# Attention scores of a decoder layer as pairs of 64-row products instead of stacked 128-row products

## The chip, the core and the metric

One core of a Trainium2 chip runs the whole program. The time is that of one execution on the device, in microseconds (us); the figure for a kernel is the median of its runs. TensorE is the matrix engine, VectorE and ScalarE work on tiles of 128 partitions, GpSimd does lighter vector work, and SP and ScalarE issue most of the transfers (DMA). In the profile they are PE (products), PEld (loads of the stationary operand into PE), DVE, ACT, POOL and SP.

## The reference

One layer of a hybrid decoder for a prompt of 512 tokens and 8 single new tokens, width 1024, 16 heads of 64, all in 32-bit floats. The part that matters here is the prompt's attention with a forget gate:

```
s = einsum("bqhd,bkhd->bhqk", q_i, k) * scale          # scale = 64 ** -0.5
s = s + fq_i[..., None] - Fk[:, :, None, :]            # sums of log forget gates
s = where(kpos <= qpos, s, -inf)                       # causal
p = softmax(s, axis=-1)
o = einsum("bhqk,bkhd->bqhd", p, v)
```

q, k and v are products of the normed input h with columns of w_in. Around this stand a recurrent branch A with its projection w_proj_a, attention of the new tokens over a paged cache, a merge, and a gated feed-forward part.

## The kernel before

Everything lies transposed: features on partitions, tokens (512 of the prompt and 8 new ones, NP and NT = 520) along the free axis. A 32-bit product is made of three cheaper ones: each operand x is split into a rounded part hi and a rest lo = x - hi, and w·a is taken as whi·ahi + wlo·ahi + whi·alo (part_product, line 305). The tokens are cut in two halves of 260 columns (HALVES). A projection (product, line 326) makes 8 x 3 products of 260 columns for each half and gives the half to a function that empties the PSUM bank. TensorE has 8 such banks; scores, transposes and projections all draw from them. Tiles in SBUF mostly come from one heap of 60 slots.

Attention goes through 8 head pairs i. The heads of a pair lie one above the other in one 128-partition tile: head a has the 64 partitions HEADS[a] of q and k.

- k_product(i) (line 1265) projects k. For head a it makes a tile ks[a] of 128 partitions: the rounded part of k on the head's own 64 partitions (line 1273, two casts per half), the rest k - hi on the other 64 (line 1277, two subtractions per half). Line 1274 copies k out for storing.
- q_load(i) (line 1285) fetches q from a scratch area in device memory: for each head its 64 rows go to both halves of a tile, four transfers of 64 partitions, on SP's queue.
- q_split(i) (line 1291) makes from each head's doubled tile a rounded part qq[a] and a rest ql[a], scaled by -1/8: two ScalarE and two VectorE instructions of 128 x 512.
- scores(i, blocks) (line 1349) makes, for a query block b of 128 tokens and each head, one score tile of 128 x (128 b + 128) in a bank of its own. Since qq[a] holds the rounded q twice and ks[a] holds k's rounded part and rest, the product of 128 rows qq·ks (line 1362) is qhi·khi + qhi·klo; the second, ql·ks (line 1363), adds qlo·khi + qlo·klo. VectorE then adds the decay rows and takes the minimum (line 1369), ScalarE the exponential (line 1370), VectorE the reciprocal of the sums (line 1372), and ScalarE or GpSimd scales (line 1376).
- turn(i, a) (line 1378) transposes the probabilities (line 1385) and splits them (lines 1389, 1390); values(i) (line 1409) multiplies with v (line 1419).

The order is written out by hand. In the loop of line 1503, step i does the k product of pair i + 1 with the turns of v's tokens between its halves, the first turn of pair i, then the v product of i + 1, with turn(i, 1) and scores(i + 1, (0, 1)) between its halves, then values(i) and scores(i + 1, (2, 3)). Between these, `at` (line 1499) issues work for the new tokens: reads of cache pages, products of their probabilities with cached values (line 946, four tiles of 32 columns of the array side by side), and small steps of their softmax. Scores of pair 0 stand inside and behind branch A's last projection (lines 1489, 1493); k_product(0) and q_load(0) stand before branch A's projections (lines 1480, 1481), and q_split(0) inside them. Weights are split a given time ahead of their use (split_upto, line 226): a cast on ScalarE (line 250) and a subtraction on VectorE (line 252). Pages of cached keys are multiplied and summed on VectorE (lines 857, 858).

Two other forms of product matter. lru_gates of the recurrent branch (line 1121) already uses row tiles: each of two heads' 64 rows has an array tile of its own, named by tile_position (line 1130). And the products of line 946 use column tiles.

Of the kernel before, what the change touches and what calls it, by code (L numbers as in the profile page):

```python
# [8 lines left out]
F32 = mybir.dt.float32  # L9
F32R = mybir.dt.float32r  # L10
I32 = mybir.dt.int32
AF = mybir.ActivationFunctionType
ALU = mybir.AluOpType
# [5 lines left out]
NP = 512  # L19
# [3 lines left out]
DH = 64  # L23
# [44 lines left out]
def kernel(ctx, tc, xT, par1, par, gates, b_f, cst, cse, own, cache_k, cache_v, cache_lf, pt,  # L68
# [3 lines left out]
    pe, act, dve, pool, sp = nc.tensor, nc.scalar, nc.vector, nc.gpsimd, nc.sync  # L72
# [9 lines left out]
    def slot(name, cols=NT, dt=F32, parts=128):  # L82
        return heap.tile([parts, cols], dt, name=name, tag="slot")

    def bank(name, parts=128, cols=512):
        return psp.tile([parts, cols], F32, name=name, tag="bank")

    def small(name, parts, cols, bufs=4):
        return sm.tile([parts, cols], F32, name=name, tag="s_" + name, bufs=bufs)
# [73 lines left out]
    for jt in range(FF // 128):  # L163
# [5 lines left out]
        for name in BLOCKS:  # L169
            units.append((c, name, 4))  # L170
            if name in JOIN[jt]:
                g, i = JOIN[jt][name]
# [12 lines left out]
    state = {"n": 0, "dma": 0, "split": 0, "load": 22, "lead": 11, "due": 0, "age": 1}  # L185
# [5 lines left out]
    def store_now(dst, src):  # L191
        act.dma_start(dst, src)
# [133 lines left out]
    def product(name, a, evac, mid=None, inside=None):  # L326
        n = begin()
        for j in range(2):
            b = bank(f"{name}_{j}")
            half_product(n, j, a, b, None if j else inside)  # L330
            evac(j, b[:, :HALF])
            if j == 0 and mid is not None:
                mid()
        run_later(n)
# [174 lines left out]
    def keep_busy(m, n, f=0):  # L509
        for _ in range(n):  # L510
            with tc.issue_after(m.ins) if m is not None else nullcontext():
                m = pe.matmul(idle[:, :HALF], lhsT=ones, rhs=x[f][:, :HALF], start=True, stop=True)
        return m
# [38 lines left out]
    def q_load(kp, raw, g3):  # L552
        sp.dma_start(raw, w_in[256 * kp:256 * kp + 256, COL_Q + 128 * g3:COL_Q + 128 * g3 + 384]
                     .rearrange("(k p) c -> p k c", p=128))

    def q_split(kp, raw, g3, behind=(), mid=None):
        hi = wp.tile([128, 2, 384], F32R, name="whi", tag="whi", bufs=3)
        lo = wp.tile([128, 2, 384], F32R, name="wlo", tag="wlo", bufs=3)
        with ExitStack() as st:
            for b in behind:  # L560
                st.enter_context(tc.issue_after(b.ins))
            for k in range(0, 2, 1 if mid else 2):
                ks = slice(k, k + 1 if mid else 2)
                state["act"] = act.copy(hi[:, ks], raw[:, ks])
                if k:
                    st.enter_context(tc.issue_after(mid()[1].ins))
                state["last"] = dve.tensor_tensor(lo[:, ks], raw[:, ks], hi[:, ks].bitcast(F32), ALU.subtract)
        for k in range(2):
            for n in range(3):
                qw[2 * kp + k, g3 + n] = hi[:, k, 128 * n:128 * n + 128], lo[:, k, 128 * n:128 * n + 128]  # L570
# [23 lines left out]
    m = None  # L594
    for f in range(KT):
        t = slot("sq1")
# [5 lines left out]
        if f > 1:  # L602
            m = keep_busy(m, 1, f)
# [43 lines left out]
    for n in range(6):  # L647
        t0, t1 = HALVES[n % 2]
# [19 lines left out]
    for n in range(6):  # L668
        t0, t1 = HALVES[n % 2]
# [176 lines left out]
    def key_sum():  # L846
        _, s, j, pg, q, half = pend.pop(0)
        r = s // 2
        c = 256 * (r % 2) + 32 * j + H * (s % 2)
        with tc.issue_after(state["last"].ins):  # L850
            if half is not None:
                b, c = 8 * (r % 2) + j, H * (s % 2) + 8 * half
                dve.tensor_tensor(pg, pg, q.unsqueeze(1).to_broadcast([128, 2, 512]), ALU.mult)
                last = dve.tensor_reduce(S[r // 2].rearrange("p (b c) -> p b c", c=32)[:, b:b + 2, c:c + 8],
                                  pg.rearrange("p j (h d) -> p j h d", d=DH), AX.X, ALU.add)
            else:
                dve.tensor_tensor(pg, pg, q, ALU.mult)  # L857
                last = dve.tensor_reduce(S[r // 2][:, c:c + H], pg.rearrange("p (h d) -> p h d", d=DH), AX.X, ALU.add)  # L858
        summed[r] += 1
        if summed[r] == 2 * NPAGE:  # L860
            chains.append([9, past_softmax(r)])
        return last
# [121 lines left out]
    qd = drp.tile([KT, 128, NT], F32, name="qd")  # L984
# [44 lines left out]
    for i in range(KT):  # L1029
        if i % 4 == 0:  # L1030
            qtp.append(bank(f"qt{i}", NS))
        if i < 6:
            t = qpart[i]
            for j, (t0, t1) in enumerate(HALVES):
                if i < 3:
                    b = qbanks[2 * i + j]
                else:
                    b = bank(f"q{i}_{j}")
# [10 lines left out]
        else:  # L1049
            t = slot("q")  # L1050
# [41 lines left out]
    HEADS = (slice(0, DH), slice(DH, 2 * DH))  # L1092
# [159 lines left out]
    sc = prm[:, :, P_SC:P_SC + 24].rearrange("p k (s n) -> p k s n", n=3)  # L1252
# [10 lines left out]
    kvs = [dict() for _ in range(KT)]  # L1263

    def k_product(i, mid=None, keys=None):
        t = slot("kt")
        ks = slot("ksA", NP, F32R), slot("ksB", NP, F32R)

        def evac(j, b):
            t0, t1 = HALVES[j]  # L1270
            n = min(t1, NP) - t0
            for a, pr in enumerate(HEADS):
                act.copy(ks[a][pr, t0:t0 + n], b[pr, :n])
            act.copy(t[:, t0:t1], b)
            for a, pr in enumerate(HEADS):
                with tc.issue_after(keys.ins) if keys else nullcontext():
                    dve.tensor_tensor(ks[a][HEADS[1 - a], t0:t0 + n], b[pr, :n], ks[a][pr, t0:t0 + n].bitcast(F32),
                                      ALU.subtract)

        product(f"k{i}", h, evac, mid)  # L1280
        kvs[i]["k"] = ks
        pool.tensor_tensor(qk8[:, NS * i:NS * i + NS], t[:, NP:], q8[:, NS * i:NS * i + NS], ALU.mult)
        store_now(kT[128 * i:128 * i + 128, :], t)

    def q_load(i):
        kvs[i]["qr"] = slot("qA", NP), slot("qB", NP)
        for a, pr in enumerate(HEADS):
            for to_ in HEADS:
                sp.dma_start(kvs[i]["qr"][a][to_], qd[i, pr, :NP])

    def q_split(i):
        qq = slot("qqA", NP, F32R), slot("qqB", NP, F32R)
        ql = slot("qlA", NP, F32R), slot("qlB", NP, F32R)
        for a in range(2):
            t = kvs[i]["qr"][a]
            act.activation(qq[a], t, AF.Copy, scale=-(DH ** -0.5))
            state["last"] = dve.scalar_tensor_tensor(ql[a], t, -(DH ** -0.5), qq[a].bitcast(F32), ALU.mult, ALU.subtract)
        del kvs[i]["qr"]
        kvs[i]["q"] = qq, ql

    def v_product(i, mid=None):
# [45 lines left out]
            fbs[hd] = f0[:, 128 * a:128 * a + 128], fmb[:, 0::3], fm[:, :384], fb  # L1347

    def scores(i, blocks):
        ks = kvs[i]["k"]  # L1350
        qq, ql = kvs[i]["q"]
        mus = small("mu", 128, 12, 4).rearrange("p (c b a) -> p c b a", c=3, b=2)
        for b in blocks:
            n = 128 * b
            for a, pr in enumerate(HEADS):
                hd = 2 * i + a
                if b == 0:
                    prob[hd] = []
                    t3 = slot("p3", 512), slot("p02", 512), slot("p1", 256)
                    pts[hd] = (t3[1][:, :128], t3[2], t3[1][:, 128:], t3[0])  # L1360
                sc = bank(f"sc{hd}_{b}")
                pe.matmul(sc[:, :n + 128], lhsT=qq[a][:, n:n + 128], rhs=ks[a][:, :n + 128], start=True, stop=False)
                pe.matmul(sc[:, :n + 128], lhsT=ql[a][:, n:n + 128], rhs=ks[a][:, :n + 128], start=False, stop=True)
                p = pts[hd][b]
                mu = mus[:, :, b - blocks[0], a]
                ins = p[:, :n + 128], sc[:, :n + 128]
                if b == 1:
                    ins = [t.rearrange("p (b c) -> p b c", b=2) for t in ins]
                dve.tensor_tensor_reduce(ins[0], fbs[hd][b], ins[1], 1.0, 3.0e38, ALU.add, ALU.min, mu[:, 0:1])  # L1369
                act.activation(p[:, :n + 128], p[:, :n + 128], AF.Exp, bias=mu[:, 0:1], scale=-1.0, accum_out=mu[:, 1:2])  # L1370
                prob[hd].append((p, mu))
        state["sums"] = dve.reciprocal(mus[:, 2], mus[:, 1])  # L1372
        for b in blocks:
            for a in range(2):
                p, mu = prob[2 * i + a][b]
                (pool.tensor_scalar(p, p, mu[:, 2:3], None, ALU.mult) if a and i + 1 < KT else act.activation(p, p, AF.Copy, scale=mu[:, 2:3]))  # L1376
# [102 lines left out]

    k_product(0)  # L1480
    q_load(0)
    decay_load(0)
    sp.dma_start(convT, conv_out)
# [19 lines left out]
    for i in range(KT):  # L1503
        last = i + 1 == KT
# [23 lines left out]
        keys = None  # L1528
        if pend:
            keys = key_sum()  # L1530
# [304 lines left out]
    for j in range(2):  # L1835
        for m in range(2 * PLAIN):
            if j == 0:
                begin(u + 3)
            b = bank(f"fi{m}_{j}")
# [90 lines left out]
```

## Time and profile before

| | |
|---|---|
| median of 3 runs | 1006.28 us (1006.1 to 1007.87) |
| the profiled execution | 1006.54 us |
| its span in the profile | 1004.9 us |
| granted TensorE clock | 0.997 |
| DMA | 206.14 MB, mean 205 GB/s |
| score products (lines 1362 and 1363) | 128, in 16 groups |

The span is the time between the first and the last instruction that the profile holds. A row of the order of time reads: start, length, engine, line, operation, output <- inputs, shape of the array that the product uses (rows * columns), shape of the moving operand, count; a bracket gives the idle time before it and what ended it. Names are the program's, with the numbers of buffers left out: sc is a score bank, ptt the transposed probabilities, pv the new tokens' value product, pa branch A's projection. Lengths of products overlap, since they are pipelined: what a product takes from TensorE's time is the step from its start to the next one's.

### The profile page before, as it was taken

To read this page: it belongs to the slowest core of one execution; us is meant where nothing else is said; L and a number is where in the kernel's file an instruction comes from. 1 tells how busy PE (TensorE), PEld (TensorE's weight loads), DVE (VectorE), ACT (ScalarE), POOL (GpSimd) and SP (SyncE) were. 2 spreads that over 40 slices of the span, in tenths; PEclk is the share of its full clock that TensorE was granted. 3 is DMA by queue.
4 is the path that set the end of the run, shared out by engine and by line. 5 is a ranking of instruction groups with operands and counts; after the bars stand their busy time and mean duration, and the time that the engine had idled before them with its cause. 6 is when DMAs were issued, how large, how long until landed. Compare 5 with 4: busy or idle time off the path is not lost.

```text
span 1004.9 us, 21556 instructions
## 1 busy us (share of the span) xinstructions
PE 985.6 (98%) x8092; PEld 915.8 (91%) x8092; DVE 791.2 (79%) x1410; ACT 564.7 (56%) x1165; POOL 339.3 (34%) x436
## 2 busy tenths in 40 slices
PE   6999999999999999999999999999999999999996
PEld 4899999999899988888888888999999999999996
DVE  5598999979999888887665444869887888888864
ACT  5434769776952587777882233544444444445453
POOL 0254121323243255654400002494343442434112
PEclk9999999999999999999999999999999999999998
DMA  9989756889879999997767994332424243233222
GB/s 315 335 271 299 235 186 184 278 261 287 277 237 378 326 311 286 303 295 231 240 223 260 333 342 139 83 106 83 117 74 126 71 120 106 64 106 106 64 64 86
DMA packets 165915, 206.14 MB, mean 205 GB/s; under 512 B 10018, under 2 KB 128434, under 8 KB 165746
## 3 DMA queue, kind: packets, MB, share of 16 engines
q1 hardware_dynamic: 149570, 153.24, 48.9%
q0 software_dynamic: 12560, 45.10, 13.4%
q10 hardware_dynamic: 3680, 6.42, 1.7%
q8 instruction: 63, 1.03, 0.4%
q14 instruction: 42, 0.34, 0.1%
HBM read 191.64 MB, written 13.09 MB: 204 GB/s over the span
## 4 chain that ended last, share of the span: by engine, by line
PE 91%; ACT 4%; DVE 2%; DMA 2%; SPq 1%; issue 1%; POOL 0%; POOLq 0%; DVEq 0%; ACTq 0%
PE fo L311 13%; PE wo L311 5%; PE gb L311 5%; PE xr L311 5%; PE pb L311 4%; PE k L311 4%; PE ga L311 4%; PE pa L311 4%; PE v L311 4%; PE gr L311 3%; PE pv L946 3%; PE po L1419 2%; PE ada L378 2%; PE ptt L1385 2%; PE fi L311 1%; PE qc L577 1%
## 5 line engine op out<-in xcount | busy, mean ns | idle before, releaser
L250 ACT CAST whi<-wraw 128x1024 fp32r<-128x1024 f32 (+1 forms) x79 | 82.0, 1040 | 96.1 <-PE pb L311 34.3
L252 DVE TENSOR_TENSOR wlo<-wraw,whi 128x1024 fp32r<-128x1024 f32 (+1 forms) x79 | 99.3, 1257 | 19.5 <-ACT whi L250 17.0
L311 PE MATMUL fo<-ach,wb 128*128 128x260 f32 x512 | 93.5, 283 | 0.0
L274 ACT CAST wb<-ws 128x512 fp32r<-128x512 f32 x72 | 44.7, 621 | 86.6 <-PE fo L311 60.2
L311 PEld LDWEIGHTS fo<-ach,wb 128*128 128x128 f32 x512 | 78.9, 188 | 0.0
L275 DVE TENSOR_TENSOR wb<-wraw,wb 128x512 fp32r<-128x512 f32 x86 | 73.8, 858 | 5.2 <-ACT wb L274 4.7
L275 DVE TENSOR_TENSOR wb<-ws,wb 128x512 fp32r<-128x512 f32 x72 | 66.2, 920 | 14.1 <-ACT wb L274 12.5
L265 POOL TENSOR_TENSOR ws<-wraw 128x512 f32<-128x512 f32 x18 | 24.6, 1367 | 152.6 <-DMA wraw<-in_w_fi_dram 95.4
L311 PE MATMUL fo<-acl,wb 128*128 128x260 f32 x256 | 72.3, 282 | 0.0
L794 POOL DMA_DIRECT2D pg<-in_cache_k_dram x70 | 37.8, 540 | 100.8 <-DVE S L858 55.3
L274 ACT CAST wb<-wraw 128x512 fp32r<-128x512 f32 x86 | 53.6, 623 | 31.0 <-ACT cp L1817 6.1
L857 DVE TENSOR_TENSOR pg<-pg,qb 128x1024 f32<-128x1024 f32 x48 | 58.5, 1233 | 0.8 <-DMA pg<-in_cache_k_dram 0.8
L1376 POOL TENSOR_SCALAR p<-p,mu 128x128 f32<-128x128 f32 (+3 forms) x28 | 39.2, 1411 | 55.3 <-DVE mu L1372 46.2
L858 DVE TENSOR_REDUCE S<-pg 128x16 f32<-128x1024 f32 x48 | 57.4, 1210 | 0.2
L311 PEld LDWEIGHTS fo<-acl,wb 128*128 128x128 f32 x256 | 48.3, 189 | 0.0
L1370 ACT ACTIVATE p<-p,mu 128x128 f32<-128x128 f32 (+3 forms) x64 | 35.3, 553 | 18.9 <-DVE mu L1369 18.6
L311 PE MATMUL v<-hh,whi 128*128 128x260 f32 x128 | 37.5, 293 | 1.0 <-DVE S L914 0.5
L311 PE MATMUL gb<-hh,whi 128*128 128x260 f32 x128 | 37.4, 292 | 0.0
L311 PE MATMUL k<-hh,whi 128*128 128x260 f32 x128 | 37.3, 292 | 0.0
L311 PE MATMUL pb<-oh,whi 128*128 128x260 f32 x128 | 37.1, 289 | 0.2 <-ACT oh L1477 0.2
L311 PE MATMUL pa<-gh,wlo 128*128 128x260 f32 x128 | 36.3, 284 | 0.8 <-DVE wlo L252 0.8
L311 PE MATMUL ga<-hh,whi 128*128 128x260 f32 x128 | 36.6, 286 | 0.4 <-ACT tA L1192 0.4
(1129 smaller groups left out, 3956.1 us busy)
## 6 DMA issues: line engine op xcount, KB each, us to landing
wraw<-in_w_fi_dram SPq DMA_DIRECT2D x44, 512.0 KB, 4.1
pg<-in_cache_k_dram POOLq DMA_DIRECT2D x42, 512.0 KB, 5.6
pg<-in_cache_v_dram SPq DMA_DIRECT2D x42, 512.0 KB, 5.3
araw<-in_ada_w_dram SPq DMA_DIRECT2D x38, 512.0 KB, 6.8
wraw<-in_w_in_dram SPq DMA_DIRECT2D x28, 512.0 KB, 6.6
wraw<-in_w_in_dram SPq DMA_DIRECT2D x11, 1024.0 KB, 8.6
pg<-in_cache_v_dram POOLq DMA_DIRECT2D x22, 512.0 KB, 6.2
wraw<-in_w_fo_dram SPq DMA_DIRECT2D x16, 512.0 KB, 5.3
```

The source lines that it names most:

```text
L250: state["act"] = act.copy(hi[:, :k1 - k0], src)
L252: state["last"] = dve.tensor_tensor(lo[:, :k1 - k0], src, hi[:, :k1 - k0].bitcast(F32), ALU.subtract)
L265: pool.tensor_tensor(s1, a21, a22, ALU.add)
L274: state["act"] = act.copy(t[:, :4], src)
L275: state["last"] = dve.tensor_tensor(t[:, 4:], src, t[:, :4].bitcast(F32), ALU.subtract)
L311: state["mm"] = pe.matmul(out[:, :t1 - t0], lhsT=wt[k], rhs=at, start=k == 0 and m == 0, stop=k == nk - 1 and m == 2)
L794: done.append(eng.dma_start(pg, cache[bass.ds(r, 1), :, c0:c1].rearrange("a p c -> (a p) c")))
L857: dve.tensor_tensor(pg, pg, q, ALU.mult)
L858: last = dve.tensor_reduce(S[r // 2][:, c:c + H], pg.rearrange("p (h d) -> p h d", d=DH), AX.X, ALU.add)
L946: pe.matmul(pv[0][32 * gq:32 * gq + 32, :], lhsT=pw[r][:, c:c + 32], rhs=pgs[gq // 2][:, 512 * hf:512 * hf + 512], start=j == 0, stop=j == ...
L1370: act.activation(p[:, :n + 128], p[:, :n + 128], AF.Exp, bias=mu[:, 0:1], scale=-1.0, accum_out=mu[:, 1:2])
L1376: (pool.tensor_scalar(p, p, mu[:, 2:3], None, ALU.mult) if a and i + 1 < KT else act.activation(p, p, AF.Copy, scale=mu[:, 2:3]))
```

## The change

k and q are split where they lie. k_product makes one rounded tile kh and one rest kl of 128 partitions, both heads at once. q_load is one transfer of 128 partitions into one tile, and q_split makes one qq and one ql. scores takes for each block both heads' banks, and makes three products per head of 64 rows each, qq·kh, qq·kl and ql·kh, heads alternating, head a on the array's row tile at 64 a. The term qlo·klo is no longer made.

```diff
 def k_product(i, mid=None, keys=None):
     t = slot("kt")
-    ks = slot("ksA", NP, F32R), slot("ksB", NP, F32R)
+    ks = slot("kh", NP, F32R), slot("kl", NP, F32R)
 
     def evac(j, b):
         t0, t1 = HALVES[j]
         n = min(t1, NP) - t0
-        for a, pr in enumerate(HEADS):
-            act.copy(ks[a][pr, t0:t0 + n], b[pr, :n])
+        act.copy(ks[0][:, t0:t0 + n], b[:, :n])
         act.copy(t[:, t0:t1], b)
-        for a, pr in enumerate(HEADS):
-            with tc.issue_after(keys.ins) if keys else nullcontext():
-                dve.tensor_tensor(ks[a][HEADS[1 - a], t0:t0 + n], b[pr, :n], ks[a][pr, t0:t0 + n].bitcast(F32),
-                                  ALU.subtract)
+        with tc.issue_after(keys.ins) if keys else nullcontext():
+            dve.tensor_tensor(ks[1][:, t0:t0 + n], b[:, :n], ks[0][:, t0:t0 + n].bitcast(F32), ALU.subtract)
...
 def q_load(i):
-    kvs[i]["qr"] = slot("qA", NP), slot("qB", NP)
-    for a, pr in enumerate(HEADS):
-        for to_ in HEADS:
-            sp.dma_start(kvs[i]["qr"][a][to_], qd[i, pr, :NP])
+    kvs[i]["qr"] = slot("qr", NP)
+    sp.dma_start(kvs[i]["qr"], qd[i, :, :NP])
 
 def q_split(i):
-    qq = slot("qqA", NP, F32R), slot("qqB", NP, F32R)
-    ql = slot("qlA", NP, F32R), slot("qlB", NP, F32R)
-    for a in range(2):
-        t = kvs[i]["qr"][a]
-        act.activation(qq[a], t, AF.Copy, scale=-(DH ** -0.5))
-        state["last"] = dve.scalar_tensor_tensor(ql[a], t, -(DH ** -0.5), qq[a].bitcast(F32), ALU.mult, ALU.subtract)
-    del kvs[i]["qr"]
+    t, qq, ql = kvs[i].pop("qr"), slot("qq", NP, F32R), slot("ql", NP, F32R)
+    act.activation(qq, t, AF.Copy, scale=-(DH ** -0.5))
+    state["last"] = dve.scalar_tensor_tensor(ql, t, -(DH ** -0.5), qq.bitcast(F32), ALU.mult, ALU.subtract)
     kvs[i]["q"] = qq, ql
...
 def scores(i, blocks):
-    ks = kvs[i]["k"]
+    kh, kl = kvs[i]["k"]
     qq, ql = kvs[i]["q"]
...
     for b in blocks:
         n = 128 * b
-        for a, pr in enumerate(HEADS):
-            hd = 2 * i + a
+        scs = [bank(f"sc{2 * i + a}_{b}") for a in range(2)]
+        for m, (qt, kt) in enumerate(((qq, kh), (qq, kl), (ql, kh))):
+            for a, pr in enumerate(HEADS):
+                pe.matmul(scs[a][:, :n + 128], lhsT=qt[pr, n:n + 128], rhs=kt[pr, :n + 128], start=m == 0,
+                          stop=m == 2, tile_position=(DH * a, 0))
+        for a in range(2):
+            hd, sc = 2 * i + a, scs[a]
...
-            sc = bank(f"sc{hd}_{b}")
-            pe.matmul(sc[:, :n + 128], lhsT=qq[a][:, n:n + 128], rhs=ks[a][:, :n + 128], start=True, stop=False)
-            pe.matmul(sc[:, :n + 128], lhsT=ql[a][:, n:n + 128], rhs=ks[a][:, :n + 128], start=False, stop=True)
```

## Prediction

> **What bounds the kernel now.** I read the page first (busy shares, then the chain that ended last), then busy time by stage, TensorE's waits in the stages that the change touches, and last the order of time of single products. The page:
>
> ```profile
> PE 985.6 (98%) x8092; PEld 915.8 (91%) x8092; DVE 791.2 (79%) x1410; ACT 564.7 (56%) x1165; POOL 339.3 (34%) x436
> ```
>
> Busy time by stage; columns are window, length, then busy us of PE, PEld, DVE, ACT and POOL, granted clock, DMA share, GB/s. The first row is the stretch of k_product(0) and of branch A's projection, the second the seven head pairs of attention:
>
> ```profile
> 286.00:338.00 52.00, 51.23 (x413) 47.24 (x412) 50.87 (x66) 14.37 (x21) 17.03 (x32) 1.00 0.94 321
> 338.00:510.00 172.00, 170.91 (x1312) 146.26 (x1311) 133.79 (x298) 131.18 (x329) 83.93 (x119) 1.00 0.87 275
> ```
>
> TensorE's waits from 286 to 510 us, all of them:
>
> ```profile
> PE pa L311 <- DVE wlo L252: 0.8, 2, 0.5
> PE v L311 <- DVE S L914: 0.5, 1, 0.5
> PE v L311 <- ACT row L926: 0.5, 2, 0.2
> ```
>
> So TensorE sets the pace: in attention it is idle for 1.1 of 172 us, while VectorE and ScalarE are idle for about 40. Work taken off VectorE, ScalarE or the DMA queues is worth only what these three lines hold. One reservation: from 286 to 338 us VectorE is busy for 50.87 of 52 us, and there TensorE waits for it. The change must be priced as TensorE's own time, then as these waits.
>
> **The products.** Scores are made in 16 visits: for each of 8 head pairs one visit for query blocks 0 and 1 (products of 128 and 256 columns) and one for blocks 2 and 3 (384 and 512). Each block now takes four products of 128 rows, one after another; afterwards it takes three pairs of 64-row products. The trace already has row tiles of 64: lru_gates makes its products so. One visit of it, twelve products in six pairs, between products of the whole array (start, length, count):
>
> ```profile
> 105.44 0.28 PE L311 MATMUL ga<-hl,whi 128*128 128x260 f32 x1
> 105.66 0.51 PE L1130 MATMUL gate<-xch,gws 64*128 64x260 f32 x4
> 106.00 0.28 PE L1130 MATMUL gate<-xcl,gws 64*128 64x260 f32 x2
> 106.12 0.40 PE L1130 MATMUL gate<-xch,gws 64*128 64x260 f32 x4
> 106.36 0.28 PE L1130 MATMUL gate<-xcl,gws 64*128 64x260 f32 x2
> 106.57 0.39 PE L311 MATMUL gb<-hh,whi 128*128 128x260 f32 x1
> 106.79 0.28 PE L311 MATMUL gb<-hh,wlo 128*128 128x260 f32 x1
> 106.92 0.28 PE L311 MATMUL gb<-hl,whi 128*128 128x260 f32 x1
> ```
>
> Two things are read from it. The groups of two take 0.28 us together, as one product does: a pair costs one product, and pairs follow each other at 0.12 us (106.00 to 106.12), the step of whole-array products too (106.79 to 106.92 is 0.13, rounded). And a visit costs extra: 0.22 us from 105.44 to 105.66 in place of 0.12, 0.34 for the first two pairs in place of 0.24, 0.21 from 106.36 to 106.57, and 0.22 for the first step after it. That is a drain of about 0.09 on each side and, on each side, one weight load of 0.11 that nothing covers: 0.40 us a visit.
>
> Now a first visit as it is, with the last transpose before it and the first product of v behind it:
>
> ```profile
> 380.98 0.27 PE L1385 MATMUL ptt<-cs,p 128*128 128x128 f32 x1
> ...
> 381.26 0.27 PE L1362 MATMUL sc<-ksB,qqB 128*128 128x128 f32 x1
> 381.38 0.27 PE L1363 MATMUL sc<-ksB,qlB 128*128 128x128 f32 x1
> ...
> 381.90 0.28 PE L1363 MATMUL sc<-ksB,qlB 128*128 128x256 f32 x1
> 382.02 0.28 PE L311 MATMUL v<-hh,whi 128*128 128x260 f32 x1
> ```
>
> It takes 1.04 us from 380.98 to 382.02. The step at 128 columns is 0.11 to 0.12, about a weight load, though it has half the columns of a 256-column one; pairing helps there only by the count, three steps for four. Afterwards: 0.20 to enter (a transpose step of 0.11 and the drain), 0.11 for the first load, three steps of 0.11, three of 0.12, 0.09 to drain: 1.08, and 0.10 for the first load of v. Together 1.18, so **0.14 more** than now. What is saved, a quarter of the products, is less than the entry and exit.
>
> A second visit and the value products (of 32 columns of the array, a different shape again) behind it:
>
> ```profile
> 387.37 0.39 PE L1362 MATMUL sc<-ksA,qqA 128*128 128x384 f32 x1
> ...
> 387.77 0.34 PE L1362 MATMUL sc<-ksB,qqB 128*128 128x384 f32 x1
> 387.94 0.34 PE L1363 MATMUL sc<-ksB,qlB 128*128 128x384 f32 x1
> ...
> 388.59 0.39 PE L1362 MATMUL sc<-ksB,qqB 128*128 128x512 f32 x1
> 388.82 0.40 PE L1363 MATMUL sc<-ksB,qlB 128*128 128x512 f32 x1
> ```
>
> ```profile
> 389.14 1.07 PE L946 MATMUL pv<-pg,pw 128*32 128x512 f32 x8
> 390.14 0.39 PE L311 MATMUL k<-hh,whi 128*128 128x260 f32 x1
> 390.37 0.28 PE L311 MATMUL k<-hh,wlo 128*128 128x260 f32 x1
> ```
>
> The steps are 0.17 and 0.23, and 388.82 to 389.14 is 0.32: here the exit's drain of 0.09 is already paid, because another shape follows, and pv pays its own way out (390.14 to 390.37 is 0.23). Now 0.11 to enter and 1.77 from 387.37 to 389.14, 1.88. Afterwards 0.20 to enter, 0.11 for the first load, three steps of 0.17, three of 0.23, 0.09 to leave: 1.61 to 1.62. That is **0.26 less**.
>
> The sum over 16. Second visits: six are followed by pv, 6 x 0.26 = 1.56 less; two are followed by k and pay a drain and a load more, so 0.26 less 0.20 is 0.06 less each: 1.7 less, and I take 1.6 because one of them comes from branch A's products with a longer entry. First visits: four sit between whole-array products, 4 x 0.14 = 0.56 more; two are followed by the small product of the softmax sums (32 columns of the array), whose drain is paid already, and come out even or 0.05 less; one has a short wait inside, which the longer entry covers, and I take it as even; the last is this one, where TensorE stood until VectorE had read a bank:
>
> ```profile
> 450.43 0.68 DVE L952 TENSOR_TENSOR dr<-pv,pvm 128x512 f32<-128x512 f32 x1
> ...
> 451.17 0.19 PEld L1362 LDWEIGHTS sc<-ksB,qqB 128*128 128x128 f32 x1 [0.30 <-DVE dr L952]
> ```
>
> Its 0.30 goes if VectorE is earlier by as much (next part), and with it the load that the wait left uncovered: 0.4 less. First visits together: 0.56 - 0.10 - 0.40, nothing. Products: **1.6 us less**. Two prices stand on a neighbouring row. That pairs overlap at 384 and 512 columns is shown at 260 only; pv's eight products of 512 columns in 1.00 us (389.14 to 390.14) are tiles that overlap at that length, so I take full overlap. Ends: no overlap, which the rivals price, and, at best, entries as cheap as now, 16 visits x about 0.2 = 3.2 us better than the sum.
>
> A rule of the Trainium skill speaks against the change at the first of these rows. By "TensorE: Matmul & The Clock Gate", under "The mechanism" of part 3, a weight load overlaps products in flight only when its row group is another; consecutive pairs here use the same two groups, so by it each pair would pay its load. The gate rows disagree: pairs 0.12 apart have no room for a load of 0.11 beside a stream of 0.12. By the rule the sum would come out slower (a rival below); I go by the rows.
>
> **Splits, loads and waits.** Per head pair the change takes these away (mean ns behind the bar, two forms each):
>
> ```profile
> L1277 DVE TENSOR_TENSOR ksB<-k,ksB 64x260 fp32r<-64x260 f32 (+1 forms) x14 | 6.0, 426 | 0.2
> L1320 DVE TENSOR_TENSOR v<-vt,v 128x256 fp32r<-128x256 f32 x14 | 6.0, 425 | 0.4
> ```
> ```profile
> L1273 ACT CAST ksB<-k 64x260 fp32r<-64x260 f32 (+1 forms) x14 | 5.2, 369 | 0.2
> ```
>
> 64 and 128 partitions cost the same 0.42, so two subtractions in place of four save 0.85 us of VectorE, and two casts fewer save 0.74 of ScalarE; one of two q splits goes on each engine too. On SP's queue three of four q loads go (a quarter MB less to move, 128 partitions x 512 x 4 bytes). None of it is on the path in attention, by the waits above. Their cover is TensorE's own work; they count at nothing, except in two places. One is the bank at 451.17. The other is here:
>
> ```profile
> 289.95 0.42 DVE L1277 TENSOR_TENSOR ksA<-k,ksA 64x260 fp32r<-64x260 f32 x1
> ...
> 291.27 0.42 DVE L1277 TENSOR_TENSOR ksB<-k,ksB 64x252 fp32r<-64x252 f32 x1
> 291.72 2.36 DVE L857 TENSOR_TENSOR pg<-pg,qb 128x1024 f32<-128x1024 f32 x2
> 294.00 2.34 DVE L858 TENSOR_REDUCE S<-pg 128x16 f32<-128x1024 f32 x2
> 296.25 1.22 DVE L252 TENSOR_TENSOR wlo<-wraw,whi 128x1024 fp32r<-128x1024 f32 x1
> ```
> ```profile
> 296.79 0.51 PE L311 MATMUL pa<-gh,whi 128*128 128x260 f32 x2
> 297.52 0.38 PE L311 MATMUL pa<-gh,wlo 128*128 128x260 f32 x1 [0.23 <-DVE wlo L252]
> ```
>
> VectorE runs without a gap from the four k subtractions to the weight split that TensorE waits for. With 0.85 us less, the split ends at 296.62 instead of 297.47 and the product can start when the one before it lets it, about 0.4 earlier (297.52 against 296.79 plus two steps, the first 0.22 behind pv), with the load then covered: **0.5 us less**. If the pages multiplied at 291.72 land no earlier, this is nothing. The waits for S and row stay: they hang on chains that the change does not shorten.
>
> One wait is added. A pair needs both of its banks before its first product, where now the second bank is needed two products later, 0.22 us. TensorE itself is queued behind it, and with it everything. At the two entries that I added a drain of 0.09 and a load of 0.11 stand in that place, so I count nothing.
>
> Sum: 1.6 + 0.5 = 2.1 us less. The profiled execution took 1006.54 (span 1004.9 and 1.6 around it), so it would take 1004.4; the median of 1006.28 lies 0.26 below that execution, so **1004.2 us**. A change under 0.2% (2.0 us) is about what a measurement of this kernel can't tell from none, and the forecast lies on that edge.
>
> **Rivals.** *The side gains don't come (1005.0 to 1006.3).* The page wait holds VectorE, the bank at 451 stays, or first visits wait for their second bank: 1.6 or less is left, and a wait of 0.2 in each of 8 first visits would take all of that. For it: banks are already short at 451. Against: each bank of k is read for 0.42 less.
>
> *More is gained (about 1002).* Entries cost less than at the gates, since loads of the next shape could be fetched while transposes run, or the waits for S and row (1.0 together) go as VectorE runs ahead. For it: the waits are there. Against: every change of shape quoted above pays the same.
>
> *Loads are not covered (1011), slower.* Place: every pair behind the first of a visit. Then a step is load plus stream: 0.11 + 0.06 (half of a 256-column stream, an estimate), 0.11 + 0.12, + 0.17, + 0.23. First visits gain 3 x 0.06 + 3 x 0.11, less the 0.11 that the first sum had for running one load ahead, so 0.4; second visits 5 x 0.11 = 0.54; 8 x 0.94 = 7.5 less the rounding, about 7 us, to 1011. It decides from somewhat over half of a load per pair, when 4.1 us are lost and the time is 2.0 above now. The gates speak against it. The rule of the Trainium skill cited above is what would bring this case.
>
> *The pairs don't overlap (about 1019).* The change then doesn't do what it says: six steps for four. Steps double, first visits 3 x 0.23 and second 3 x 0.40 more, 8 x 1.9 = 15. Against: the groups of two in 0.28.
>
> **How the numbers follow.** Forecast 0.47, with its own range 1003.2 to 1005.2, of which 0.29 lies beyond 2.0 us and 0.18 within. Side gains lost 0.27, within. More gained 0.17, faster. Loads uncovered 0.04, no overlap 0.02, and 0.03 for bank waits in many visits that pass 4 us: slower 0.09. Faster 0.29 + 0.17 = 0.46, same 0.18 + 0.27 = 0.45, slower 0.09. The range of 8 in 10, 1001.6 to 1006.8, takes in the side cases to their ends and leaves out the slower ones and the tail of the gains.
>
> **What would show it.** In the new profile: pairs of sc products in 64 rows starting together, 0.17 and 0.23 apart in second visits; 1.08 from the last transpose to v's first product in first visits and 0.22 for v's first step; 1.62 from the last po product to pv; no wait of pa for wlo at 297 and none for dr near 451. The prediction is wrong if pairs are 0.2 or more apart at 128 columns, if sc products wait for ScalarE or VectorE in several visits, or if the time moves outside 286 to 510 us.

## The result and the profile after

The changed kernel takes 1005.17 us (median of 22 runs, 1004.56 to 1005.97) against 1006.63 us (22 runs, 1005.67 to 1010.4) for the kernel before: ratio 0.9982, 95% interval [0.9976, 0.9989]. The medians differ by 1.46 us; the ratio makes it about 1.8. Run once more, beside other kernels (e13 below), it was 1005.46 us against 1005.89, ratio 0.9993 [0.9984, 1.0002]. So the gain is small: by the ends of the two intervals between 0.2 us lost and 2.4 us gained. The profiled execution took 1004.86 us, its span is 1003.2 us, its granted clock 0.997.

The page's line of busy times:

```profile
PE 985.0 (98%) x8156; PEld 912.4 (91%) x8156; DVE 775.6 (77%) x1386; ACT 555.5 (55%) x1141; POOL 342.8 (34%) x436
```

64 products were added (8092 to 8156), 24 instructions each went from VectorE and ScalarE. The two stretches, columns as in the prediction:

```profile
286.00:338.00 52.00, 51.46 (x421) 47.58 (x420) 49.26 (x68) 12.53 (x19) 18.22 (x31) 1.00 0.96 332
338.00:510.00 172.00, 170.35 (x1390) 142.30 (x1389) 119.74 (x273) 125.86 (x313) 83.67 (x119) 1.00 0.82 263
```

And TensorE's waits from 286 to 525 us, all of them:

```profile
PE ptt L1378 <- ACT p L1369: 1.5, 2, 0.9
PE pa L311 <- DVE wlo L252: 0.5, 1, 0.5
```

The wait of pa for wlo at 297 is gone, and so are v's waits for S and row (0.5 each). A new one of 1.5 has come: transposes of the probabilities wait for ScalarE, in the last pair. A second visit, for the one shown at 387.37 before:

```profile
385.79 0.27 PE L1412 MATMUL po<-pl,v 128*128 128x128 f32 x1
385.99 0.44 PE L1349 MATMUL sc<-kh,qq 64*128 64x384 f32 x2
386.27 0.34 PE L1349 MATMUL sc<-kl,qq 64*128 64x384 f32 x2
386.45 0.34 PE L1349 MATMUL sc<-kh,ql 64*128 64x384 f32 x2
386.62 0.39 PE L1349 MATMUL sc<-kh,qq 64*128 64x512 f32 x2
386.85 0.39 PE L1349 MATMUL sc<-kl,qq 64*128 64x512 f32 x2
387.08 0.40 PE L1349 MATMUL sc<-kh,ql 64*128 64x512 f32 x2
```

The count of 2 is a pair; its two products start within 10 ns of each other. Entry 0.20, first load 0.11 (0.28 to the second pair in place of 0.17), then 0.17 and 0.23. The next instruction, pv, starts 1.617 after the last po, where the prediction has 1.62.

Where the time went is read from the starts of four products in the order of time: the first pa of branch A's projection, the first sc, the first vt of the last pair, the first po of the last pair. The columns are the lengths between them in us, start to pa first; "all back" and "without overlap" are kernels of the next section.

| profile | to pa | pa to sc | sc to vt | vt to po | po to end |
|---|---|---|---|---|---|
| before | 289.14 | 49.16 | 170.91 | 14.20 | 481.48 |
| after | 288.18 | 48.61 | 168.35 | 15.91 | 482.16 |
| after, second profile | 288.66 | 48.67 | 168.18 | 15.90 | 482.37 |
| before, products alone changed (all back) | 288.91 | 49.78 | 170.10 | 15.91 | 483.29 |
| all back, second profile | 288.22 | 49.65 | 170.70 | 15.86 | 483.17 |
| before, splits and loads alone changed | 289.73 | 48.01 | 169.22 | 14.24 | 482.05 |
| after, without overlap | 288.64 | 48.44 | 184.33 | 13.96 | 482.64 |
| after, last turns later | 288.76 | 48.39 | 168.10 | 13.99 | 482.61 |
| that, pv behind the scores | 288.93 | 48.21 | 166.19 | 13.98 | 483.04 |

In the three middle columns, all that the change touches, after is 0.55 + 2.56 - 1.71 = **1.4 us** shorter than before. In the outer columns TensorE runs the same products in all kernels, and yet they differ by up to 1.6 and 1.8. Most of the first is the wait for the first transfer (5.8 to 7.4 us), which is chance: it differs by 1.3 between the two profiles of all back. The last column is not chance. From the po that begins it to the first r3p, a small product near the end, the two profiles of after take 474.80 and 474.81 us, the two of all back 475.83 and 475.82, before 474.12. So it belongs to the program: after loses 0.7 us there and all back 1.7. TensorE waits for 1.4 to 1.5 us there in all five; the rest is slightly longer steps between the same products, and why was not traced.

### The profile page after: what moved, and what is told of

It is laid out like the page before. It is cut to its first block, busy times and chain, and to the rows that moved or that the text cites. A ratio compares the mean times of both kernels' runs of the same rounds, so it can differ in the third digit from the quotient of the medians.

```text
span 1003.2 us, 21579 instructions
## 1 busy us (share of the span) xinstructions
PE 985.0 (98%) x8156; PEld 912.4 (91%) x8156; DVE 775.6 (77%) x1386; ACT 555.5 (55%) x1141; POOL 342.8 (34%) x436
## 4 chain that ended last, share of the span: by engine, by line
PE 91%; ACT 4%; DVE 2%; DMA 1%; issue 1%; SPq 0%; POOL 0%; DVEq 0%; ACTq 0%
PE fo L311 13%; PE wo L311 5%; PE pa L311 5%; PE xr L311 5%; PE pb L311 4%; PE gb L311 4%; PE v L311 4%; PE k L311 4%; PE ga L311 4%; PE gr L311 4%; PE pv L946 3%; PE po L1412 2%; PE sc L1349 2%; PE ada L378 2%; PE ptt L1378 2%; PE fi L311 1%
## 5 line engine op out<-in xcount | busy, mean ns | idle before, releaser
L252 DVE TENSOR_TENSOR wlo<-wraw,whi 128x1024 fp32r<-128x1024 f32 (+1 forms) x79 | 97.2, 1230 | 18.4 <-ACT whi L250 15.8
L275 DVE TENSOR_TENSOR wb<-wraw,wb 128x512 fp32r<-128x512 f32 x86 | 77.1, 896 | 5.5 <-ACT wb L274 4.6
L275 DVE TENSOR_TENSOR wb<-ws,wb 128x512 fp32r<-128x512 f32 x72 | 62.5, 868 | 13.8 <-ACT wb L274 12.1
L1369 POOL TENSOR_SCALAR p<-p,mu 128x128 f32<-128x128 f32 (+3 forms) x28 | 34.4, 1240 | 61.5 <-DVE mu L1365 50.3
L311 PE MATMUL xr<-hh,whi 128*128 128x260 f32 x128 | 36.9, 288 | 0.0
```

What stands on the lines that cost most here:

```text
L252: state["last"] = dve.tensor_tensor(lo[:, :k1 - k0], src, hi[:, :k1 - k0].bitcast(F32), ALU.subtract)
L275: state["last"] = dve.tensor_tensor(t[:, 4:], src, t[:, :4].bitcast(F32), ALU.subtract)
L311: state["mm"] = pe.matmul(out[:, :t1 - t0], lhsT=wt[k], rhs=at, start=k == 0 and m == 0, stop=k == nk - 1 and m == 2)
```

## The experiments

Every kernel ran beside the kernel before; ratios are to it. Three groups of runs were made: e1, e2, e4 and e7 beside 1006.43 us, e3, e5, e8 and e9 beside 1006.25, e10 to e13 beside 1005.89.

**e1, the products alone.** k's casts and subtractions, q's split and q's loads are per head again, the spare transfers into a tile that nothing reads:

```diff
-            act.copy(ks[0][:, t0:t0 + n], b[:, :n])
+            for pr in HEADS:
+                act.copy(ks[0][pr, t0:t0 + n], b[pr, :n])
...
-        sp.dma_start(kvs[i]["qr"], qd[i, :, :NP])
+        spare = slot("qr2", NP)
+        for t in (kvs[i]["qr"], spare):
+            for pr in HEADS:
+                sp.dma_start(t[pr], qd[i, pr, :NP])
```

> Row-tile products as in the changed kernel, but k is cast and subtracted head by head (two casts and two subtractions of 64 partitions per half), q is split head by head and q is fetched in four transfers: VectorE, ScalarE and SP do about the work of the kernel before. The result is the reference's. Theory A (TensorE's own time in the 16 visits is worth 1.3 to 1.8 us, the lighter VectorE another 1.5, and a changed order of the last pair's transposes costs 1.7): 1.3 saved, 1.7 lost, so about 0.4 us above before, 1007.0; visits take 1.09 and 1.62 us as in the changed kernel, and the waits for wlo near 297 us and for the bank near 450 are back. Theory B (all of the gain is the lighter VectorE, the products come out even): 1.7 us above before, 1008.3. Theory C (the products are all of the gain): as the changed kernel, 1005.2.

1009.68 us, 1.0034 [1.0022, 1.0047]: slower than before, by more than any theory had. The visits are nearly as in after (22.0 us in all for 21.7), so the products gain, but the waits are back and worse.

**e2, splits and loads alone.** The kernel before with its four products of 128 rows; head 1's products read head 0's tiles, and head 1's own splits and loads are left out.

```diff
-            for a, pr in enumerate(HEADS):
-                act.copy(ks[a][pr, t0:t0 + n], b[pr, :n])
+            pr = HEADS[0]
+            act.copy(ks[pr, t0:t0 + n], b[pr, :n])
```

> The kernel before with its stacked 128-row products, two per head and block, but head B is computed from head A's tiles: one cast and one subtraction of k per half, one q split, one q transfer. Left out: the splits and loads of every second head, so the scores of these heads are those of their neighbours. Theory A: only VectorE's waits go (0.4 before the weight split, 0.4 to 0.7 at the bank near 450 us, 0.6 behind it), so 1.2 to 1.6 us below before, 1005.1 to 1005.5, with the order of the last pair's transposes as before. Theory B: about 3 us below before, 1003.5, since the order that costs 1.7 is not there. Theory C: as before, 1006.6.

1003.97 us, 0.9974 [0.9965, 0.9983], nearest to B. Of TensorE's waits from 286 to 524 us one line is left:

```profile
PE pa L311 <- DVE wlo L252: 0.4, 1, 0.4
```

So the new splits and loads are worth 2.5 us by themselves, with no product changed: pa to sc is 1.15 shorter than before, sc to vt 1.69. Not all of this is the lighter load of the engines: 1.0 us, v's waits, goes by another way, shown in the next section.

**e4, the last pair's turns one step later** (after otherwise): turn(7, 0) stands where turn(7, 1) stood, and turn(7, 1) behind it.

```diff
         def mid_a():
             v_tokens(i)
-            if last:
-                turn(i, 0)
...
-            if not last:
-                turn(i, 1)
+            turn(i, 1)
...
-        turn(i, 1 if last else 0)
+        turn(i, 0)
```

> The changed kernel with the last pair's two turns moved one step later, to where the other pairs have them. Theory A: the transposes no longer stand 1.5 us for ScalarE's scaled probabilities, 1.5 to 1.7 us below the changed kernel, 1003.5, and 3.2 below before. If that wait is only moved (VectorE's splits of the probabilities come later and values waits for them): as the changed kernel, 1005.2.

1003.76 us, 0.9973 [0.9963, 0.9983]. ptt's wait for p is gone, the last pair takes 13.99 in place of 15.91: A.

**e7, e4 and pv right behind the first score visit**, so that one exit from row tiles leads into column tiles and not into whole products:

```diff
-    VALUES_AT = [(1, 1, 0, 1)] * 4 + [(1, 1, 0, 0)] + [(1, 1, 0, 1)] * 2 + [(1, 1, 0, 0)]
+    VALUES_AT = [(1, 0, 1, 1)] * 4 + [(1, 0, 1, 0)] + [(1, 0, 1, 1)] * 2 + [(1, 1, 0, 0)]
```

> As the run with the later last turns, and one of the value products of the new tokens (tiles of 32 columns) per pair moved from behind the first turn to right behind the first score visit, so that the way out of the row tiles and the way into the column tiles are one change of the array's shape. Theory A: 0.20 us less for each of seven pairs, 1.4 less, so 1002.2. If a change between two tiled shapes costs as much as two changes, or the value pages and their chain are late in that place: 1003.5 or above.

1001.66 us, 0.9954 [0.9941, 0.9968], 2.1 below e4: A, by somewhat more than its 1.4. sc to vt is 1.9 shorter. This version beats both kernels, the one before by 4.8 us.

**e3, head by head.** The two loops around the products are exchanged, so that TensorE's queue holds a block's three products of head 0 and then three of head 1 (in the program as it is built, too).

```diff
-            for m, (qt, kt) in enumerate(((qq, kh), (qq, kl), (ql, kh))):
-                for a, pr in enumerate(HEADS):
+            for a, pr in enumerate(HEADS):
+                for m, (qt, kt) in enumerate(((qq, kh), (qq, kl), (ql, kh))):
```

> The kernel after with the six products of a block in another order: all three of head 0, then all three of head 1. Same products, same tiles. Theory A (the change pays because two neighbours in different row halves run at the same time): only the last product of head 0 and the first of head 1 still run together, so two of three pairs fall apart. A pair's step is 0.06 to 0.07 us at 128 columns, 0.115 at 256, 0.17 at 384, 0.23 at 512, 0.58 for the four blocks, 1.75 us for the three pairs of each of eight turns: two thirds of 8 x 1.75 are 9.4 us, all of them 14. Expected 1014.5 us, between 1013 and 1019. Theory B (what the visits gained comes from the loads or the order of the queue, not from the products' overlap): as the kernel after, 1005.2 us.

1005.24 us, 0.999 [0.9981, 0.9999]: theory A is wrong as it was put, and 1005.2 was B's number. But the order of time shows what neither said:

```profile
500.52 0.45 PE L1349 MATMUL sc<-kh,qq 64*128 64x384 f32 x2
500.80 0.35 PE L1349 MATMUL sc<-kl,qq 64*128 64x384 f32 x2
500.98 0.35 PE L1349 MATMUL sc<-kh,ql 64*128 64x384 f32 x2
501.15 0.40 PE L1349 MATMUL sc<-kh,qq 64*128 64x512 f32 x2
```

The pairs stand as before: kh·qq of both heads within 10 ns, though two products of head 0 lie between them in the queue. The overlap doesn't depend on who is the neighbour in the queue.

**e10, one row tile.** To take the overlap away, both heads' products read the first 64 rows and use the first row tile; the second head's own scores are left out.

```diff
-                    pe.matmul(scs[a][:, :n + 128], lhsT=qt[pr, n:n + 128], rhs=kt[pr, :n + 128], start=m == 0,
-                              stop=m == 2, tile_position=(DH * a, 0))
+                    pe.matmul(scs[a][:, :n + 128], lhsT=qt[HEADS[0], n:n + 128], rhs=kt[HEADS[0], :n + 128],
+                              start=m == 0, stop=m == 2, tile_position=(0, 0))
```

> The kernel after with the products of both heads on the first 64 rows of q and k, all in one row tile; left out are the second head's own scores, so its softmax works on the first head's. As many products of the same size, but no two in different row tiles. Theory A (two row tiles run at the same time, a pair costs one product, in whatever order the queue holds them): each pair now costs two, and a 128-column product no less than a weight load lets it, about 0.11 us; 3 x (0.11 + 0.115) more in each first visit and 3 x (0.17 + 0.23) in each second, 1.9 us a pair of heads, 15 in eight: 1020 us, between 1015 and 1022. Theory B (a pair costs no less than two products by themselves; the order by heads changed nothing because there is nothing to lose): 1005.2 us.

1019.51 us, 1.0126 [1.0111, 1.0142]: A. A visit's products in its order of time:

```profile
514.76 0.61 PE L1349 MATMUL sc<-kh,qq 64*128 64x384 f32 x2
515.22 0.52 PE L1349 MATMUL sc<-kl,qq 64*128 64x384 f32 x2
515.58 0.51 PE L1349 MATMUL sc<-kh,ql 64*128 64x384 f32 x2
515.93 0.62 PE L1349 MATMUL sc<-kh,qq 64*128 64x512 f32 x2
```

Two products of 384 columns now need 0.35, twice 0.17. All 16 visits, from the instruction ahead to the one behind, take 36.9 us in place of 21.7, 15.2 more. Together with e3: overlap is what carries the change, and it belongs to the row tile and not to the order.

**e5, the move of e4 in the kernel before.**

> The kernel before with the two turns of the last pair one step later, the move that took the kernel after from 1005.2 to 1003.8 us. Theory A (the move only mends the order in which the kernel after came to run its last transposes; the kernel before had them between the products of gb already): the last pair takes 14.0 instead of 14.2 us, the kernel 1006.2 us, between 1005.9 and 1006.6. Theory B (the move is a gain of its own, whatever stood there): 1005.0 us, 1.4 less than the kernel before.

1007.05 us, 1.0005 [0.9996, 1.0014], the last pair 14.00 in place of 14.20: the move is no gain of its own, B is out. e4's gain is the mending of what the change had upset.

**e8, e9, e11: the three parts of e1 one at a time, and e12, e1 again; e13, the kernel after again.** e8 has the first two changed lines of e1's diff and the like for the subtraction, e9 the last four, e11 this:

```diff
-        act.activation(qq, t, AF.Copy, scale=-(DH ** -0.5))
+        for pr in HEADS:
+            act.activation(qq[pr], t[pr], AF.Copy, scale=-(DH ** -0.5))
```

> The kernel after with k's casts and subtractions made per head again, two and two of 64 partitions, 16 more on ScalarE and 16 more on VectorE; q stays split at once. All splits and loads back cost 4.5 us over the kernel after (1009.7 against 1005.2). Theory A (VectorE's order around the weight split and the softmax's S and row is what the change relieves): this one has most of it back, 1008.3 us, between 1007.3 and 1009.7, with pa waiting for wlo again and v for S or row. Theory B (q's transfers and its splits are what counts): 1005.2 to 1005.7 us.

> The kernel after with q loaded by four transfers of 64 rows a pair again, two of them into a spare tile that nothing reads; all splits stay whole. Theory A (VectorE's order is what the change relieves; q's loads are early enough): as the kernel after, 1005.2 us, within 0.4. Theory B (SyncE's queue and the DMA traffic of q count): 1007 us or more, a half of the 4.5 us that all splits and loads back cost.

> The kernel after with q split per head, two casts and two subtractions of 64 partitions a pair; k's splits and q's load as in the kernel after. Of the 4.5 us that all three cost together, k's splits alone showed about 1.3 and q's loads alone about 1.0. Theory A (the three add up): the rest, 2.2 us, 1007.4 us, with v waiting for row or S again. Theory B (each by itself finds slack, only together they are late): 1005.2 to 1006.0 us.

> The same kernel as the one with all splits and loads back, beside the parts of it on one chip. Theory A (its 4.5 us over the kernel after are a cost of the work): 1009.7 us again, within 0.6. Theory B (a part was chance of that program's runs, such as the VectorE operation of 4.48 us beside GpSimd): 1007.5 us or less.

> The kernel after once more, as the measure for the other three on this chip and for what two profiles of one program differ by. Theory A (the start's transfer and the feed-forward steps vary by chance): 1005.2 us, within 0.5; the wait for the first transfer anywhere from 5.8 to 7.4 us, and the stage behind the last po within 481.5 to 483.3. Theory B (they belong to the program): 6.0 and 482.2 again, within 0.2.

| kernel | us | ratio, interval |
|---|---|---|
| e8, k's splits back | 1006.46 | 0.9999 [0.999, 1.0008] |
| e9, q's loads back | 1006.16 | 0.999 [0.998, 1.0001] |
| e11, q's splits back | 1005.78 | 0.9995 [0.9986, 1.0004] |
| e12, all back | 1010.05 | 1.0038 [1.0024, 1.0052] |
| e13, after | 1005.46 | 0.9993 [0.9984, 1.0002] |

Kernels with after's splits and loads ran beside them: e3 beside e8 and e9, e13 beside the others. Over these e8 costs 1.2 us, e9 0.9 and e11 0.3 by the medians (0.9, 0.0 and 0.2 by the ratios): 2.5 at most in sum, where e12, all three together, costs 4.6, of which 1.0 lies behind the last po. e12 takes A: it is no chance. e11 takes B; e8 and e9 lie between their theories. e13 takes A for the time of the kernel and for the first wait, 6.5 where it had been 6.0; its last column, 482.37 for 482.16, is what B said. TensorE's waits in e12 from 286 to 525 us:

```profile
PE ptt L1384 <- ACT p L1375: 1.5, 2, 0.9
PE pa L311 <- DVE wlo L252: 1.4, 2, 0.9
PE v L311 <- DVE S L914: 0.5, 1, 0.5
PE v L311 <- ACT row L926: 0.5, 2, 0.2
```

Two places of this cost were found here, a third in the next section (v's waits). In e8, e1 and e12, and in none of the eleven other profiles, one VectorE addition of the new tokens' softmax (line 895) is held for three to four us. Its two instructions in after and in e12, with GpSimd's first instruction of decay_rows (in e12 also the last) and the next of VectorE:

```profile
299.46 0.69 DVE L895 TENSOR_TENSOR S<-S,suf 128x128 f32<-128x128 f32 x2
300.67 0.41 POOL L1334 COPY fm<-fb 128x256 f32<-128x256 f32 x1
```
```profile
300.08 4.78 DVE L895 TENSOR_TENSOR S<-S,suf 128x128 f32<-128x128 f32 x2
300.52 0.41 POOL L1340 COPY fm<-fb 128x256 f32<-128x256 f32 x1
...
304.15 0.45 POOL L1342 TENSOR_TENSOR fb<-fb,cs 128x128 f32<-128x128 f32 x1
304.78 0.42 DVE L1196 TENSOR_TENSOR tA<-pa,tA 128x260 f32<-128x260 f32 x1
```

In after the pair is done 0.52 before GpSimd begins. In e12 the second one lies beside GpSimd's ten instructions and ends only when they have ended. The weight split behind it on VectorE is then late, and pa waits 0.9 for it. That is a step, not a slope: k's four subtractions at 288 us take 1.74 in place of 0.74 for two, and line 895 comes to lie beside GpSimd's work. The kernel before makes the same four subtractions, but there GpSimd's next instruction begins at 302.61, 0.41 after the pair is done. The second place is the page of cached values near 369 us. In e9:

```profile
369.08 1.05 PE L946 MATMUL pv<-pg,pw 128*32 128x512 f32 x4
370.42 1.05 PE L946 MATMUL pv<-pg,pw 128*32 128x512 f32 x4 [0.29 <-DMA pg<-in_cache_v_dram]
```

In after all eight of these products start together and take 1.07; here the second four wait for their page, 1.33 lost. Transfers of pages issued from 345 to 372 us, with KB and median us to landing, in after and e9:

```profile
pg<-in_cache_v_dram SPq DMA_DIRECT2D x8, 512.0 KB, 5.2
```
```profile
pg<-in_cache_v_dram SPq DMA_DIRECT2D x7, 512.0 KB, 6.7
```

With four transfers of q in place of one a page lands 1.5 us later: the median is 6.0 to 6.9 in the five kernels with four, and 4.2 to 5.6 in those with one, e7 apart, which reads pages at other times (6.4). The kernel before has the four too, but reaches this place at 370.85, 1.8 us later, and doesn't wait. What else the parts cost together was not traced to one of them.

## Why the prediction was right, and where not

The time, 1005.17 for 1004.2, lies in the range; the change of 0.18% falls on the near side of 0.2%, where the forecast stood on the far side. The sum of 2.1 us became 1.4 in the stretch, by errors in both directions: visits 1.8 less, wlo 0.5, v's waits 1.0, the last pair 1.7 more, together 1.6 less. That the time came within 1 us of the forecast is in part luck, since the two largest errors, 1.0 and 1.7, stand against each other.

*Second visits, -1.6: right*, -1.67 with the first step behind them. 1.617 to 1.632 from the instruction ahead to the next one; no pair is more than 10 ns apart at 384 or 512 columns.

*First visits, sum nothing: nearly right*, -0.14. 1.083 to 1.090 for the predicted 1.08, v's first step 0.22 to 0.225. At 450 us the bank's wait went, worth 0.53 for the predicted 0.4, and by the way that was predicted: the last score tile uses pv's bank in both kernels, and VectorE has read it (line 952) by 445.21 in after, well before the visit begins at 447.99. All visits together, between the neighbours, went from 24.12 to 21.69 us. The weight loads are covered, as the gate rows had it: pairs on the same two row tiles follow each other at 0.17 and 0.23. The rule of the Trainium skill ("TensorE: Matmul & The Clock Gate", "The mechanism"), by which loads overlap only with another row group, isn't what these rows show.

*wlo at 297, -0.5: right*, 0.47; pa to sc is 0.55 shorter. This also covers the page's landing, which came early enough.

*"The waits for S and row stay: they hang on chains that the change does not shorten": wrong.* They went, 1.0 us that the prediction left to a rival, and not because the chains became shorter. The end of the chain to S in the kernel before, and the product of v that waits for it:

```profile
450.43 0.68 DVE L952 TENSOR_TENSOR dr<-pv,pvm 128x512 f32<-128x512 f32 x1
451.15 0.75 DVE L954 TENSOR_TENSOR dr<-dr 128x256 f32<-128x256 f32 x2
452.04 0.42 DVE L914 TENSOR_TENSOR S<-S,lgm 128x256 f32<-128x256 f32 x1
```
```profile
452.52 0.38 PE L311 MATMUL v<-hh,whi 128*128 128x260 f32 x1 [0.51 <-DVE S L914]
```

And in after:

```profile
449.21 0.39 PE L311 MATMUL v<-hh,whi 128*128 128x260 f32 x1
450.74 0.42 DVE L914 TENSOR_TENSOR S<-S,lgm 128x256 f32<-128x256 f32 x1
```

S comes 1.5 us behind v's start now: v doesn't wait for it any more. What ties the two together is a PSUM bank. Line 914 reads the bank into which TensorE has just made lgm, a small product of the new tokens' softmax, and line 926 (row) likewise reads that of lgs. The framework gives out the banks when a program is built, and the built programs can be compared. In the kernel before, the second half of v draws the very bank of lgs or lgm in pairs 1, 5 and 6, and must wait until it is read: the three waits of the list. With all splits and loads back (e1) it does so in the same three, with q's loads alone back (e9) only in pair 6, and in after, e2, e3, e4, e8, e10 and e11 in none. Each profile has just the waits that its banks call for. So the change took these waits away by a new draw of banks, which nobody aimed at. The mistake is to have asked which operations S needs, instead of why v needs S. Shown is what the draw does; by which rule a change of splits or loads alters it was not tried.

*"None of it is on the path in attention": wrong, in the price.* Splits and loads alone are 2.5 us (e2), their loss together 4.6 (e12), when the prediction had 0.9 for them (0.5 and 0.4). 1.0 of each is the draw of banks, 1.0 of the 4.6 lies behind the last po. For the rest, VectorE's 21% of idle time is no cover for one place in its queue (line 895 in e12), and a page that just lands in time is late when it lands 1.5 us later (e9).

*The last pair: not in the sum.* +1.71 us, the largest error, and most of it within the stretch that the prediction named: it had looked at what the instructions cost there, not at whether their order stays. The instructions of this stretch are the same; the order in which the framework's scheduler queues them is not. Before, the transposes of turn(7, 0) were spread:

```profile
509.64 0.49 PE L1385 MATMUL ptt<-cs,p 128*128 128x128 f32 x3
510.06 1.06 PE L946 MATMUL pv<-pg,pw 128*32 128x512 f32 x8
510.95 0.55 PE L1435 MATMUL sn<-qk,cs 128*16 128x8 f32 x16
512.08 0.44 PE L1385 MATMUL ptt<-cs,p 128*128 128x128 f32 x2
513.20 0.55 PE L1385 MATMUL ptt<-cs,p 128*128 128x128 f32 x3
```

Afterwards all eight stand ahead of pv, and wait for ScalarE's scaling of p:

```profile
505.58 0.38 PE L1378 MATMUL ptt<-cs,p 128*128 128x128 f32 x2
506.87 0.55 PE L1378 MATMUL ptt<-cs,p 128*128 128x128 f32 x3 [0.91 <-ACT p L1369]
507.99 0.55 PE L1378 MATMUL ptt<-cs,p 128*128 128x128 f32 x3 [0.57 <-ACT p L1369]
508.46 1.06 PE L946 MATMUL pv<-pg,pw 128*32 128x512 f32 x8
```

e4 moves only these transposes and takes 1.9 us of this stretch back, 1.4 of the kernel by the medians; in the kernel before the same move brings 0.2 there (e5). So the loss hangs on the order. The order comes with the products: e1, which has them with the old splits, takes 15.91 there, e2, which has the new splits with the old products, 14.24. By which rule the scheduler chose it was not tried. And the order costs only where TensorE is ahead of ScalarE. e10 has it too, and loses nothing (13.96):

```profile
520.54 2.35 ACT L1369 ACTIVATE p<-p,mu 128x384 f32<-128x384 f32 x4 [0.24 <-DVE mu L1365]
```
```profile
521.85 1.04 PE L1378 MATMUL ptt<-cs,p 128*128 128x128 f32 x8
```

With its longer visits the transposes come 1.31 us after ScalarE has begun to scale p. In after they come at 505.58, 0.62 before it begins (506.20).

*Outside 286 to 510 us.* That the time moves there is one of the prediction's signs of being wrong. It did, by the 0.7 us that after loses behind the last po; the prediction has no term for it, and its cause is open.

*The rivals.* No overlap was put at 1019 us, 15 more for the visits; in e10 they take 15.2 more, and the kernel 1019.51, so that price was right and the case not. "Side gains don't come, 1005.0 to 1006.3" has the measured time in its range, but not by its mechanism: the side gains came, and the last pair took them. "More gained, about 1002" had one of its two ways right, the waits for S and row: without the last pair's loss, e4 is at 1003.8.

## What to carry to other kernels

Work taken off an engine that is idle 20% of the time is priced by what stands behind it in its queue, place by place: just-in-time pages, a split that TensorE waits for, an operation that must not fall beside GpSimd's. When a product waits for an operation whose result it doesn't use, ask which bank it was given. After any change to the instructions, compare the order on each engine and the banks where nothing was meant to change, above all at the last step of a loop; a 0.2% gain is easily paid back there, and easily recovered by moving one line. When the array changes its shape often, put the phases of other shapes next to each other, so that they share entries and exits.

## What the runs showed of the hardware that was not expected

Row tiles run as streams of their own here: with three products of one tile queued ahead of three of the other, the two still start within 10 ns (e3), and the two on one tile take twice the time (0.35 for two of 384 columns, e10).

Two VectorE additions with both operands in SBUF, 0.69 us together in after, took 4.78 when ten GpSimd copies and additions began beside the second (e12; 4.79 in e1; 3.96 in e8, beside eight); it ended after the last of them. The Trainium skill ("SBUF — State Buffer", "Who interferes with whom") has a VectorE instruction with two inputs in SBUF contend with a GpSimd instruction that reads SBUF; in e12 it was not one instruction that VectorE waited for, but all ten. Not every such meeting ends so: in the kernel before, the multiplication of line 857 began at 303.88 beside the same run of GpSimd and took 1.81 us, where its mean is 1.23, while one GpSimd addition took 1.44 in place of 0.46. What decides between the two was not tried.
